# RMSNorm with SiLU on one core: all block transfers through one queue, in turns of loads and stores

## The chip, the core and the metric

The kernel runs on one core of a Trainium2 chip. The core has engines that run side by side, each with its own list of instructions: VectorE (DVE in the profile), ScalarE (ACT), TensorE (PE), GpSimd (POOL) and SyncE (SP), which here only issues transfers. Data lies in HBM and is worked on in SBUF, an on-chip memory of 128 partitions; 16 DMA engines carry it between the two. A transfer is issued by an instruction on an engine's list (here SyncE's or ScalarE's), goes into that engine's DMA queue, and is then carried out while the engine goes on. An instruction that must wait for a semaphore holds up all that stands behind it on its engine.

The metric is device time in microseconds (us). A profiled execution shows every instruction and every DMA packet.

## The reference

```python
batch, seq_len, hidden = 8, 1024, 2048        # x: float32
rms = np.sqrt(np.mean(x ** 2, axis=-1, keepdims=True) + eps)
out = gamma * x / rms
return (out * (1 / (1 + np.exp(-out)))).astype(np.float32)
```

That is 8192 rows of 2048 numbers. Each row is divided by its root mean square, multiplied by gamma, and put through SiLU. 64 MiB are read and 64 MiB written.

## The kernel before

The rows are cut into 16 blocks of 512 rows (`nblk`). A block is one SBUF tile of 128 partitions with four rows each (`J = 4`): 32 KB a partition, 4 MiB in all. Partition p of block b holds four neighbouring rows, so that a block is one contiguous piece of HBM. The pool has six such tiles (`BUFS = 6`); a block is loaded into one, worked on in place, and stored from it, and the block six later takes it over when the store has landed.

The steps of a block b, with the lines of the profile:

- `load(b)`, line 54: a transfer issued by ScalarE.
- `squares_scalar(b)`, line 65, and `squares_vector(b)`, line 73: the sums of squares of its four rows, some on ScalarE (Square with a running sum), the others on VectorE (a multiply with a sum, called reduce below). `share(b)` says how many ScalarE takes: two, or one for the even blocks from 4 to 12.
- `root(b)`, line 82: Sqrt on ScalarE over the four sums. Before it ScalarE loads the table with Sqrt, unless it has it already; Square needs no other table than the one that is there.
- `invert(b)`, line 87: the reciprocal, on VectorE.
- `multiply(b)`, line 92: four instructions on VectorE, x times the row's reciprocal times gamma.
- `silu(b)`, line 98: its table, then two instructions on ScalarE, two rows each; then `store(b)`, line 102: a transfer issued by SyncE.

So loads pass through ScalarE's DMA queue (q10 in the profile) and stores through SyncE's (q1). The order on each engine is the order of the text, since the schedule is written by hand (`manual_schedule`).

The start: load 0, gamma's row (8 KB, line 110, by SyncE), load 1; TensorE spreads gamma over the partitions by a multiplication with ones (line 113), VectorE copies it to SBUF (line 115), and a small copy on ScalarE (line 116) waits for that. Behind it on ScalarE come loads 2 to 5.

The main loop, for b from 0 to 14, has three forms. In the first three turns: multiply(b), the squares of block b+1 on ScalarE, silu(b) and its store, the squares of b+1 on VectorE, root(b+1), invert(b+1). From turn 3 to 13: squares and root of b+1 first, then multiply(b), silu(b) and the store, invert(b+1). Here a load, `[b + 3]`, is issued on ScalarE after the first Square of block b+1, for blocks 6 to 15; it waits until the store of the block six before has landed. Turn 14 has the first form again. The last block's rows are multiplied by gamma alone (line 155) and the reciprocal is applied as the scale of four Silu instructions (line 157), each ready for one row; then its store.

Of the kernel before, what the change touches and what calls it, by code (L numbers as in the profile page):

```python
# [1 line left out]

# [4 lines left out]

ACT = mybir.ActivationFunctionType
ALU = mybir.AluOpType


@with_exitstack
def kernel(
    ctx: ExitStack,
    tc: tile.TileContext,
    x: bass.AP,
    gamma: bass.AP,
    eps: bass.AP,
    out: bass.AP,
):  # L20

    nc = tc.nc
    P = nc.NUM_PARTITIONS
    f32 = mybir.dt.float32
    x2 = x.flatten_outer_dims()
    o2 = out.flatten_outer_dims()  # L30
    n, d = x2.shape
    J = 4
    BUFS = 6
    nblk = n // (P * J)
    xb = x2.rearrange("(b p j) d -> b p (j d)", p=P, j=J)
    ob = o2.rearrange("(b p j) d -> b p (j d)", p=P, j=J)

    singles = ctx.enter_context(tc.tile_pool(name="singles", bufs=1))
    pool = ctx.enter_context(tc.tile_pool(name="pool", bufs=BUFS))
    small = ctx.enter_context(tc.tile_pool(name="small", bufs=2))  # L40
    psum = ctx.enter_context(tc.tile_pool(name="psum", bufs=1, space=bass.MemoryType.PSUM))

    Q = 4
    w = d // Q
    g = singles.tile([P, d], f32)
    eps_t = singles.tile([P, 1], f32)
    ones = singles.tile([P, P], f32)
    junk_a = psum.tile([P, d], f32, name="junk_a")
    junk_v = psum.tile([P, d], f32, name="junk_v")
    blocks, sss, rmss, rstds = {}, {}, {}, {}  # L50

    def load(b):
        xt = pool.tile([P, J * d], f32, name="xt")
        nc.scalar.dma_start(out=xt, in_=xb[b])  # L54
        blocks[b] = xt

    def row(b, j):
        return blocks[b][:, j * d:(j + 1) * d]

    def squares_scalar(b, loads=()):  # L60


        sss[b] = small.tile([P, J], f32, name="ss")
        for j in range(share(b)):
            nc.scalar.activation(out=junk_a, in_=row(b, j), func=ACT.Square,  # L65
                                 accum_out=sss[b][:, j:j + 1])
            if j == 0:
                for s in loads:
                    load(s)

    def squares_vector(b):
        for j in range(share(b), J):
            nc.vector.tensor_tensor_reduce(  # L73
                out=junk_v, in0=row(b, j), in1=row(b, j), scale=1.0, scalar=0.0,
                op0=ALU.mult, op1=ALU.add, accum_out=sss[b][:, j:j + 1])

    def share(b):
        return 1 if 4 <= b <= 12 and b % 2 == 0 else 2

    def root(b):  # L80
        rms = small.tile([P, J], f32, name="rms")
        nc.scalar.activation(out=rms, in_=sss.pop(b), func=ACT.Sqrt, scale=1.0 / d, bias=eps_t)  # L82
        rmss[b] = rms

    def invert(b):
        rstd = small.tile([P, J], f32, name="rstd")
        nc.vector.reciprocal(out=rstd, in_=rmss.pop(b))  # L87
        rstds[b] = rstd

    def multiply(b):  # L90
        for j in range(J):
            nc.vector.scalar_tensor_tensor(out=row(b, j), in0=row(b, j), scalar=rstds[b][:, j:j + 1],  # L92
                                           in1=g, op0=ALU.mult, op1=ALU.mult)

    def silu(b):
        for h in range(0, J, 2):
            cols = slice(h * d, (h + 2) * d)
            nc.scalar.activation(out=blocks[b][:, cols], in_=blocks[b][:, cols], func=ACT.Silu)  # L98
        store(b)

    def store(b):
        nc.sync.dma_start(out=ob[b], in_=blocks[b])

    with tc.manual_schedule():

        load(0)
        nc.vector.memset(ones, 1.0)  # L107
        nc.vector.memset(eps_t, float(eps))
        nc.scalar.activation(out=junk_a[:, 0:1], in_=ones[:, 0:1], func=ACT.Square)  # L109
        nc.sync.dma_start(out=g[0:1, :], in_=bass.AP(tensor=gamma.tensor, offset=gamma.offset, ap=[[d, 1], [1, d]]))  # L110
        for c in range(Q):
            cols = slice(c * w, (c + 1) * w)
            nc.tensor.matmul(junk_v[:, cols], ones[0:1, :], g[0:1, cols], start=True, stop=True)  # L113
        load(1)
        nc.vector.tensor_copy(out=g, in_=junk_v)  # L115
        nc.scalar.copy(out=junk_a[:, 0:1], in_=junk_v[:, d - 1:d])  # L116
        for b in range(2, BUFS):
            load(b)

        last = nblk - 1
        SOON = 3
        squares_scalar(0)
        squares_vector(0)
        root(0)
        invert(0)
        for b in range(last):
            loads = [b + 3] if BUFS <= b + 3 < nblk else []
            if b < SOON:  # L130
                multiply(b)
                squares_scalar(b + 1, loads)
                silu(b)
                squares_vector(b + 1)
                root(b + 1)
            elif b < last - 1:
                squares_scalar(b + 1, loads)
                squares_vector(b + 1)
                root(b + 1)
                multiply(b)  # L140
                silu(b)
            else:
                multiply(b)
                squares_scalar(b + 1)
                silu(b)
                squares_vector(b + 1)
                root(b + 1)
            if b + 1 < last:
                invert(b + 1)


        for j in range(J):
            if j == J // 2:
                invert(last)
            nc.vector.tensor_mul(out=row(last, j), in0=row(last, j), in1=g)  # L155
        for j in range(J):
            nc.scalar.activation(out=row(last, j), in_=row(last, j), func=ACT.Silu,  # L157
                                 scale=rstds[last][:, j:j + 1])
        store(last)


# [1 line left out]
_INS = ['x', 'gamma', 'eps']  # L163
_OUTS = [((8, 1024, 2048), 'float32')]

_NUMBERS = {'eps': 9.999999747378752e-06}


# [26 lines left out]
```

## Time and profile before

| | us |
|---|---|
| three runs: lowest, median, highest | 316.79, 317.0, 317.33 |
| profiled execution, first to last instruction (span) | 315.1 |
| median of the runs less that span | 1.9 |
| VectorE busy | 235.3 (75%) |
| ScalarE busy | 213.9 (68%) |
| PE busy | 7.2 (2%) |
| moved by DMA | 134.24 MB, 426 GB/s over the span |
| a load from issue to landing, median | 38.7 |
| a store from issue to landing, median | 29.0 |

The profile's page gives, for each engine, its busy time, and for 40 equal slices of the span the busy tenths of each engine, the busy share of the 16 DMA engines, and the rate of the packets that start in the slice. Its chain is the work that ended last, followed back from the end: at each step to what released it. Groups of instructions are shown with line, engine, operation, output<-inputs, shapes and count, then busy time, mean ns of one, the idle time of the engine just before them and what ended it. Windows give busy times and the DMA rate of chosen stretches, in us from the span's start; packets are counted in the window in which they start.

### The profile page before, as it was taken

What the parts mean: (1) busy time and instruction counts of PE and PEld (TensorE: products, weight loads), DVE (VectorE), ACT (ScalarE), POOL (GpSimd) and SP (SyncE); (2) the same over time, 40 slices, a digit from 0 to 9 for tenths busy, and PEclk for the clock granted to TensorE, in tenths of its full rate; (3) what the DMA queues carried; (4) which work ended last, traced back from release to release, by engine and by line L of the source; (5) the groups of instructions that cost most, each with busy time, mean ns of one, the idle gap of its engine ahead of it and who ended that gap; (6) DMA issues with size and microseconds to landing.
All of it is one profiled execution on the core that took longest, in us unless ns stands there. A gap on an engine that the chain in (4) does not pass through costs nothing.

```text
span 315.1 us, 439 instructions
## 1 busy us (share of the span) xinstructions
PE 7.2 (2%) x8; PEld 2.5 (1%) x8; DVE 235.3 (75%) x157; ACT 213.9 (68%) x137; POOL 0.2 (0%) x4
## 2 busy tenths in 40 slices
PE   6200000000000000000000000000000000000000
PEld 2000000000000000000000000000000000000000
DVE  0679697979895695957969489593995939999600
ACT  1269998972799258682687827877278768779910
POOL 0000000000000000000000000000000000000000
DMA  8999999999999999999999999999999999999997
GB/s 334 412 453 416 383 458 408 462 403 462 403 459 408 454 412 458 408 462 403 462 403 462 408 458 408 458 408 458 416 449 416 449 416 449 428 437 428 437 428 308
DMA packets 4613, 134.24 MB, mean 426 GB/s; under 512 B 514, under 2 KB 514, under 8 KB 514
## 3 DMA queue, kind: packets, MB, share of 16 engines
q10 hardware_dynamic: 2304, 67.11, 49.8%
q1 hardware_dynamic: 2306, 67.12, 49.3%
q14 instruction: 3, 0.02, 0.0%
HBM read 67.12 MB, written 67.11 MB: 426 GB/s over the span
## 4 chain that ended last, share of the span: by engine, by line
DMA 68%; DVE 14%; ACT 11%; issue 1%; ACTq 1%; DVEq 0%
DMA xt<-in_x_dram 68%; DVE xt L92 9%; DVE junk_v L73 5%; ACT xt L98 4%; ACT junk_a L65 3%; ACT xt L157 2%; ACT L82 1%; ACTq L190 1%; ACT L157 0%; ACT L98 0%; ACT rms L82 0%; DVE ss L73 0%; ACTq L54 0%; DVE rstd L87 0%; ACT L109 0%
## 5 line engine op out<-in xcount | busy, mean ns | idle before, releaser
L92 DVE SCALAR_TENSOR_TENSOR xt<-xt,rstd,g 128x2048 f32<-128x2048 f32 x60 | 137.0, 2346 | 0.1
L98 ACT ACTIVATE xt<-xt 128x4096 f32<-128x4096 f32 x30 | 108.3, 3615 | 27.4 <-DVE xt L92 27.4
L73 DVE CUSTOM_DVE_ANT_0 junk_v<-xt 128x2048 f32<-128x2048 f32 x37 | 85.1, 2299 | 42.9 <-DMA xt<-in_x_dram 42.2
L65 ACT ACTIVATE junk_a<-xt 128x2048 f32<-128x2048 f32 x27 | 50.7, 1876 | 16.1 <-DMA xt<-in_x_dram 14.0
L82 ACT ACT_TABLE_LOAD x15 | 19.2, 1283 | 26.6 <-DVE ss L73 26.5
L98 ACT ACT_TABLE_LOAD x14 | 18.0, 1283 | 0.2
L115 DVE COPY g<-junk_v 128x2048 f32<-128x2048 f32 x1 | 2.3, 2292 | 9.0 <-PE junk_v L113 9.0
L87 DVE RECIPROCAL rstd<-rms 128x4 f32<-128x4 f32 x16 | 2.7, 172 | 8.4 <-ACT rms L82 8.4
L155 DVE TENSOR_TENSOR xt<-xt,g 128x2048 f32<-128x2048 f32 x4 | 8.9, 2277 | 0.0
L82 ACT ACTIVATE rms<-ss,eps_t 128x4 f32<-128x4 f32 x16 | 4.8, 297 | 5.7 <-DVE ss L73 5.5
L157 ACT ACTIVATE xt<-xt,rstd 128x2048 f32<-128x2048 f32 x4 | 7.7, 1991 | 0.0
L113 PE MATMUL junk_v<-g,ones 1*128 1x512 f32 x8 | 7.2, 1072 | 2.8 <-DMA g<-in_gamma_dram 2.8
L116 ACT COPY junk_a<-junk_v 128x1 f32<-128x1 f32 x1 | 0.1, 144 | 9.8 <-DVE g L115 9.8
L73 DVE DVE_READ_ACCUMULATOR2_ANT ss<- 128x1 f32 x37 | 5.2, 141 | 0.0
L65 ACT ACTIVATION_READ_ACCUMULATOR junk_a<-xt 128x1 f32 x27 | 5.0, 186 | 0.0
L113 PEld LDWEIGHTS junk_v<-g,ones 1*128 1x128 f32 x8 | 2.5, 325 | 5.9 <-issue 5.9
L109 ACT ACT_TABLE_LOAD x1 | 1.3, 1283 | 1.1 <-PEq L176 1.1
L157 ACT ACT_TABLE_LOAD x1 | 1.3, 1283 | 0.0
L107 DVE MEMSET ones<- 128x128 f32 x1 | 0.2, 165 | 0.8 <-PEq L176 0.8
L109 ACT ACTIVATE junk_a<-ones 128x1 f32<-128x1 f32 x1 | 0.2, 174 | 0.0
L176 POOL MEMSET const-bfloat16-1.0<- 128x1 bf16 x1 | 0.1, 103 | 0.0
L176 POOL MEMSET const-uint8-127<- 128x1 uint8 x1 | 0.1, 102 | 0.0
(3 smaller groups left out, 0.3 us busy)
## 6 DMA issues: line engine op xcount, KB each, us to landing
xt<-in_x_dram ACTq DMA_DIRECT2D x16, 4096.0 KB, 38.7
out_dram<-xt SPq DMA_DIRECT2D x16, 4096.0 KB, 29.0
g<-in_gamma_dram SPq DMA_DIRECT2D x1, 8.0 KB
```

What stands on the lines that cost most here:

```text
L65: nc.scalar.activation(out=junk_a, in_=row(b, j), func=ACT.Square, accum_out=sss[b][:, j:j + 1])
L73: nc.vector.tensor_tensor_reduce(out=junk_v, in0=row(b, j), in1=row(b, j), scale=1.0, scalar=0.0, op0=ALU.mult, op1=ALU.add, accum_out=sss ...
L82: nc.scalar.activation(out=rms, in_=sss.pop(b), func=ACT.Sqrt, scale=1.0 / d, bias=eps_t)
L87: nc.vector.reciprocal(out=rstd, in_=rmss.pop(b))
L92: nc.vector.scalar_tensor_tensor(out=row(b, j), in0=row(b, j), scalar=rstds[b][:, j:j + 1], in1=g, op0=ALU.mult, op1=ALU.mult)
L98: nc.scalar.activation(out=blocks[b][:, cols], in_=blocks[b][:, cols], func=ACT.Silu)
L109: nc.scalar.activation(out=junk_a[:, 0:1], in_=ones[:, 0:1], func=ACT.Square)
L113: nc.tensor.matmul(junk_v[:, cols], ones[0:1, :], g[0:1, cols], start=True, stop=True)
L115: nc.vector.tensor_copy(out=g, in_=junk_v)
L155: nc.vector.tensor_mul(out=row(last, j), in0=row(last, j), in1=g)
L157: nc.scalar.activation(out=row(last, j), in_=row(last, j), func=ACT.Silu, scale=rstds[last][:, j:j + 1])
L190: with _tile.TileContext(nc) as tc:
```

## The change

All 32 block transfers are issued by SyncE, in an order written out in `QUEUE`: loads 0 to 5, stores 0 to 4, loads 6 to 10, stores 5 to 9, loads 11 to 15, stores 10 to 15. `transfers(done)`, called after the Silu of each block, issues the next entries of that list as far as they are loads or stores of blocks that are done in the text; each still waits on its semaphores, a store for its Silu, a load for the landing of the store that had its slot. Gamma's row is issued by ScalarE instead of SyncE. The small copy on ScalarE is gone.

The six tiles become six slots of one tile, `ring`. Blocks are paired: partition p holds eight neighbouring rows of a pair, four in the even block and four in the odd one (`view`), so that the rows of one block's neighbouring partitions stand 64 KB apart in HBM instead of 32 KB; each partition's piece is 32 KB as before.

The compute order goes by groups of blocks (0 to 5, 6 to 10, 11 to 15). The first block of a group has no look-ahead but the squares of the next on ScalarE and VectorE around its Silu; within the group the squares of block b+1 stand before the multiply of b; but the group's last block is worked on after the Silu of the one before it, except block 15. ScalarE and VectorE take two rows of squares each in every block. The small buffers for sums and roots are three instead of two.

```diff
+QUEUE = [
+    ('L', 0), ('L', 1), ('L', 2), ('L', 3), ('L', 4), ('L', 5),
+    ('S', 0), ('S', 1), ('S', 2), ('S', 3), ('S', 4),
+    ('L', 6), ('L', 7), ('L', 8), ('L', 9), ('L', 10),
+    ('S', 5), ('S', 6), ('S', 7), ('S', 8), ('S', 9),
+    ('L', 11), ('L', 12), ('L', 13), ('L', 14), ('L', 15),
+    ('S', 10), ('S', 11), ('S', 12), ('S', 13), ('S', 14), ('S', 15),
+]
+
+GROUPS = [range(0, 6), range(6, 11), range(11, 16)]
...
-    pool = ctx.enter_context(tc.tile_pool(name="pool", bufs=BUFS))
-    small = ctx.enter_context(tc.tile_pool(name="small", bufs=2))
+    small = ctx.enter_context(tc.tile_pool(name="small", bufs=3))
...
+    ring = singles.tile([P, SLOTS * J * d], f32, name="xt")
...
-    def load(b):
-        xt = pool.tile([P, J * d], f32, name="xt")
-        nc.scalar.dma_start(out=xt, in_=xb[b])
-        blocks[b] = xt
+    def rows(b, j, k):
+        at = (b % SLOTS) * J + j
+        return ring[:, at * d:(at + k) * d]
...
+    def view(t, blocks):
+
+        q = blocks[0] // 2
+        both = t[q * 2 * P * J:(q + 1) * 2 * P * J, :].rearrange("(p j) d -> p (j d)", p=P, j=2 * J)
+        at = blocks[0] % 2 * J
+        return both[:, at * d:(at + len(blocks) * J) * d]
+
+    todo = list(QUEUE)
+
+    def transfer():
+        kind, *blocks = todo.pop(0)
+        sb = rows(blocks[0], 0, len(blocks) * J)
+        if kind == "L":
+            nc.sync.dma_start(out=sb, in_=view(x2, blocks))
+        else:
+            nc.sync.dma_start(out=view(o2, blocks), in_=sb)
+
+    def transfers(done):
+
+        while todo and (todo[0][0] == "L" or todo[0][-1] <= done):
+            transfer()
...
-    def share(b):
-        return 1 if 4 <= b <= 12 and b % 2 == 0 else 2
+    def squares(b):
+        squares_scalar(b)
+        squares_vector(b)
+        root(b)
...
-        store(b)
-
-    def store(b):
-        nc.sync.dma_start(out=ob[b], in_=blocks[b])
+        transfers(b)
...
-        load(0)
+        transfer()
...
+        nc.scalar.dma_start(out=g[0:1, :], in_=bass.AP(tensor=gamma.tensor, offset=gamma.offset, ap=[[d, 1], [1, d]]))
...
-        nc.sync.dma_start(out=g[0:1, :], in_=bass.AP(tensor=gamma.tensor, offset=gamma.offset, ap=[[d, 1], [1, d]]))
...
-        load(1)
+        transfer()
         nc.vector.tensor_copy(out=g, in_=junk_v)
-        nc.scalar.copy(out=junk_a[:, 0:1], in_=junk_v[:, d - 1:d])
-        for b in range(2, BUFS):
-            load(b)
...
+        transfers(-1)
+
+        for group in GROUPS:
+            first, end = group[0], group[-1]
+            squares(first)
+            invert(first)
+            multiply(first)
+            squares_scalar(first + 1)
+            silu(first)
+            squares_vector(first + 1)
+            root(first + 1)
+            for b in group[1:-1]:
+                if b + 1 < end or end == last:
+                    squares(b + 1)
+                invert(b)
                 multiply(b)
                 silu(b)
...
+            if end < last:
+                squares(end)
+                invert(end)
+                multiply(end)
+                silu(end)
...
-        store(last)
+        transfers(last)
```

## The prediction

> **What bounds the kernel now.** I read the page's slices and queues first, then the chain that ended last, then the rate of the transfers stretch by stretch, and last the engines. The page:
>
> ```profile
> DMA  8999999999999999999999999999999999999997
> ...
> DMA packets 4613, 134.24 MB, mean 426 GB/s; under 512 B 514, under 2 KB 514, under 8 KB 514
> ...
> q10 hardware_dynamic: 2304, 67.11, 49.8%
> q1 hardware_dynamic: 2306, 67.12, 49.3%
> ...
> DMA 68%; DVE 14%; ACT 11%; issue 1%; ACTq 1%; DVEq 0%
> ...
> L92 DVE SCALAR_TENSOR_TENSOR xt<-xt,rstd,g 128x2048 f32<-128x2048 f32 x60 | 137.0, 2346 | 0.1
> L98 ACT ACTIVATE xt<-xt 128x4096 f32<-128x4096 f32 x30 | 108.3, 3615 | 27.4 <-DVE xt L92 27.4
> L73 DVE CUSTOM_DVE_ANT_0 junk_v<-xt 128x2048 f32<-128x2048 f32 x37 | 85.1, 2299 | 42.9 <-DMA xt<-in_x_dram 42.2
> L65 ACT ACTIVATE junk_a<-xt 128x2048 f32<-128x2048 f32 x27 | 50.7, 1876 | 16.1 <-DMA xt<-in_x_dram 14.0
> ```
>
> The 16 DMA engines are at 9 in every slice but the first and last; the two queues' packets take 49.8 + 49.3 = 99.1% of their span. The chain is 68% a load being waited for, and VectorE and ScalarE stand 42.2 and 14.0 us for loads. So the transfers are the bound: 16 blocks in, 16 out, 4 MiB each. The windows tell what rate they get (time, busy time of PE, PEld, DVE, ACT, POOL, clock, DMA share, GB/s):
>
> ```profile
> 4.50:34.90 30.40, 5.44 (x7) 1.66 (x5) 20.95 (x14) 17.89 (x14) 0.00 (x0) 1.00 1.00 431
> 34.90:40.75 5.85, 0.00 (x0) 0.00 (x0) 3.92 (x3) 5.77 (x8) 0.00 (x0) 1.00 0.98 358
> 40.75:279.20 238.45, 0.00 (x0) 0.00 (x0) 192.98 (x129) 167.21 (x102) 0.00 (x0) 1.00 1.00 433
> ...
> 279.20:312.00 32.80, 0.00 (x0) 0.00 (x0) 17.26 (x11) 21.56 (x13) 0.00 (x0) 1.00 1.01 435
> ```
>
> The first stretch is loads alone (the first store is issued at 35.18 in the timeline), the third is both directions at once from two queues, the last is stores alone (the last load is through at 279.2 in the chain). The three rates are the same: packets are counted where they start, and one round of 16 packets of 32 KB is 0.52 MB, 1.2 us of a stretch. Direction and number of queues do not change the rate. The one hole is the second stretch, in which the store queue starts beside the running load queue:
>
> ```profile
> DMA packets 64, 2.10 MB, mean 358 GB/s; under 512 B 0, under 2 KB 0, under 8 KB 0
> ```
>
> 2.10 MB at 433 GB/s would be 4.84 us; it took 5.85. 1.0 us is lost there, once. All the rest at 433 GB/s is 134.24 MB, 309.9 us. SyncE's wait for the last store ends at about 314.1 (the issue, the last of line 102, starts at 300.9 and is over by 301.2; the wait behind it is 12.9). 314.1 - 309.9 = 4.2 us is thus all that stands above the rate: the 1.0, some 2.5 at the start (first issue at 0.73, next to nothing moved before 1.7, and 374 GB/s from 1.7 to 4.5), and the rest the last landing.
>
> **The change, part by part**, against the profiled execution (span 315.1). The runs' median, 317.0, is 1.9 above that span; I keep the 1.9.
>
> *Bytes and packets.* 16 loads and 16 stores of 4 MiB in 32 KB pieces stay: 309.9 us at the measured rate. With one direction at a time the rows above give 431 and 435 against 433 mixed: no gain, no loss. Cost 0; the error of these windows is about one round of packets in 30 us, and the long one pins the mixed rate, so I allow 0.3% (1 us) either way for it.
>
> *The start.* Load 0 is now SyncE's first instruction; SyncE issued gamma at 0.73, the same time as ScalarE its load. Gamma goes to ScalarE's queue, ahead of its table load. 0. Loads 2 to 5 were issued at 12.38, behind ScalarE's copy; now they follow at once (six issues of about 0.4 to 0.5 us). They wait in the queue behind loads 0 and 1 either way, so nothing lands earlier. ScalarE loses the copy (0.14), the waits behind it, and its four issues (1.81): its first Square starts at about 13.0 instead of 14.29, off the path.
>
> *Does the one queue ever run dry?* SyncE issues in order, so a store that waits for its Silu holds up every later transfer. Working it out from rows: two reduces 2 x 2.4, reciprocal 0.2, four multiplies 4 x 2.35 make VectorE 14.4 a block; two Squares 4.0, two table loads 2.6, Sqrt 0.3, two Silus 7.2 make ScalarE 14.1. Load 0 lands at 0.73 + 12.2 = 12.9, and as before store 0 is ready at 35.2 (block 0 and 1 keep their order). VectorE, whose multiply of block 0 ends near 29, then does two pairs of reduces and the multiply of block 1 (end 47.9), and goes on at 14.4: stores are ready 3.7 after each multiply, at 51.6, 65.8, 80.0, and store 4 at 89.4 (block 5's reduces come after it).
> The queue: the chain has load 1 through at 22.66; with 9.69 us a block (4.194 MB at 433 GB/s) load 5 is through at 61.4, and stores 0 to 4 end at 71.1, 80.8, 90.5, 100.2, 109.9. Each must be issued about 1 us before its turn: store 3 is ready at 80.0 for 90.5, store 4 at 89.4 for 100.2. The least lead is some 10 us.
> Loads 6 to 10 wait in SyncE for their slot's store to land (71.1 to 109.9) and for store 4's issue; load 6 is queued at 90 for 109.9, load 10 at 111 for 148.6. They end at 119.6 to 158.3. Store 5 (ready at 108) is queued at 111. Block 6 landed, the same pattern as from 12.9 to 35.2 gives store 6 at 141.9, then 158.3, 172.5, and store 9 at 181.9 for its turn at 197.1. Loads 11 to 15 end at 216.4 to 255.2, stores 11 to 14 are ready at 238.7, 255.1, 269.3, 283.5 for 264.9, 274.6, 284.3, 294.0. Block 15: from 279.8 four gamma multiplies of 2.28 and four Silus of 1.99 behind them end at 292.6, for 303.7. So every wait on compute lies under a transfer of another block: 0. What covers it is the 10 us of lead; each us of lateness beyond that would be a us at the end. The look-ahead, the dropped uneven share of squares and the extra small buffers (3 for 2) act only within it.
> The last store ends at 255.2 + 6 x 9.69 = 313.3, against 314.1 now.
>
> *The hole at 34.9.* It is where the second queue starts. Now only one queue carries blocks, and its stores are queued 25 us before their turn. Bounds: it goes (-1.0), or it belongs to the first store, whichever queue, and comes again at 61 (0). I take -1.0: what is slow in that stretch is not the stores but two rounds of loads ahead of them (from 36 to 39.5 the windows have 32 packets start, all of the load queue, with 94.3% of the engines' time: 1.65 us each), and a queue's start costs something at 1.7 to 4.5 too (2.8 us x (1 - 374/433) = 0.4).
>
> *Five turns of direction* (61, 110, 158, 207, 255). No row shows a load behind a store in one queue. Lower end 0: from 40.75 to 279.2 the engines serve both queues, half and half, at the single-direction rate. Upper end: each turn costs what the hole did, 5 x 1.0 = 5.0; the 0.4 of the first start lies between, 2.0 for five. I take 0, the long row being nearest.
>
> *Addresses.* A block's partition rows are now 64 KB apart in HBM instead of 32 KB, two blocks interleaved; each piece stays 32 KB. No row has that spacing. Ends: 0, since no row shows the HBM side setting the rate; or the slowest rate of any row, 358 GB/s, throughout: 375 - 310 = +65. I take 0, by the kinship with the 32 KB pieces of all rows.
> The Trainium skill speaks against this part: "DMA: Bandwidth & Descriptors", section "Latency and other measured facts", has copies whose rows in HBM lie a large power of two apart run slower, 207 GB/s a direction at 512 KiB against 214 at full rate. By that 3% the sum would be some 10 us more, about 326; its smallest spacing is eight times the one here, and no row of this profile tests it.
>
> **Sum:** 315.1 - 1.0 + 0 + 0 = 314.1 span, 316.0 with the 1.9 around it.
>
> **The rivals.**
> A (0.45), the forecast: the hole goes, turns are free: 316.0, own range 315.6 to 316.6.
> B (0.23), the hole stays, as it belongs to the first store: 317.0. For it: it happens just when stores begin. Against: it stretches loads.
> C (0.15), on the slower side: each turn of direction in one queue empties the engines for p. The end is 316.0 + 5p; it is slower by 0.2% from p = 0.33. At 0.4 it is 318.0, at 1.0 it is 321.0. For it: the hole is the only place where a direction begins. Against: 238 us of both directions at 433.
> D (0.08), the 64 KB spacing costs rate: each 1% is 3.1 us; 319 to 326.
> E (0.05), a store comes later than its turn, because compute loses its 10 us of lead: for 2 to 4 us in one turn, 318 to 320. Against: VectorE and ScalarE now stand 42.2 and 14.0 us for loads.
> F (0.04), one direction at a time is faster than mixed: 0.5% of 309.9 is 1.5 us: 314.5. Against: 431 and 435.
>
> **How the numbers follow.** About 0.2% (0.6 us) can be told from no change. Faster: most of A (0.38) and F, 0.42. Same: the rest of A and most of B, 0.28. Slower: C, D, E and a little of B, 0.30. The range from 315.6 to 319.8 holds A, B, most of C and E and the low part of D, some 0.85; F, the far half of C and most of D lie outside.
>
> **What the profile would show.** Right: one queue with nearly all bytes, the other only gamma; 433 GB/s in each turn and no dip at 61, 110, 158, 207, 255; stores issued near 35, 52, 66, 80, 89, and the last near 293; engines' waits for loads large, with no effect. Wrong: dips at the turns (C), one near 61 only (B), a rate below 430 inside a turn (D), or a store issued after the transfer before it has ended (E).

## The result, and the profile after

The changed kernel takes 317.44 us (median of 16 runs, 317.2 to 318.13) against 317.0 before (16 runs, 316.79 to 317.33); the ratio is 1.0018, with a 95% interval of 1.0011 to 1.0024. It is slower, by 0.4 us, where 1.0 us less was forecast. The profiled execution has a span of 316.3, and it is the slowest of the 16 (318.13); the median run's span is 315.7, so 0.6 us of what its trace shows more than before is its own.

The page of the changed kernel (slices, queues, chain, groups):

```profile
DMA  8999999999999999999999999999999999999996
...
DMA packets 4612, 134.24 MB, mean 424 GB/s; under 512 B 513, under 2 KB 513, under 8 KB 513
...
q1 hardware_dynamic: 4608, 134.22, 98.9%
...
q10 hardware_dynamic: 2, 0.01, 0.0%
...
DVE 58%; DMA 25%; ACT 6%; issue 1%; DVEq 1%; ACTq 1%; SPq 0%
...
L96 DVE CUSTOM_DVE_ANT_0 junk_v<-xt 128x2048 f32<-128x2048 f32 x32 | 73.5, 2298 | 40.3 <-DMA xt<-in_x_dram 39.6
L91 ACT ACTIVATE junk_a<-xt 128x2048 f32<-128x2048 f32 x32 | 60.0, 1876 | 52.1 <-DMA xt<-in_x_dram 51.6
```

The bytes are in one queue now, and the DMA engines are as full as before. The chain names VectorE with 58%, but that is the way it is followed: a store in the queue was released by its Silu long before its turn, and the chain goes back from there. VectorE and ScalarE still stand idle 39.6 and 51.6 us for loads. The bound is the same, so the places to look are those where the engines moved less than their 433 GB/s. The windows of the changed kernel (columns as in the prediction, the last is GB/s):

```profile
4.50:58.10 53.60, 5.51 (x7) 1.66 (x5) 45.46 (x31) 39.24 (x31) 0.00 (x0) 1.00 1.00 430
58.10:61.70 3.60, 0.00 (x0) 0.00 (x0) 3.60 (x3) 3.60 (x2) 0.00 (x0) 1.00 1.00 291
61.70:154.00 92.30, 0.00 (x0) 0.00 (x0) 67.44 (x45) 66.33 (x43) 0.00 (x0) 1.00 1.01 435
154.00:162.00 8.00, 0.00 (x0) 0.00 (x0) 7.93 (x7) 7.06 (x5) 0.00 (x0) 1.00 0.98 422
162.00:250.00 88.00, 0.00 (x0) 0.00 (x0) 60.65 (x39) 59.40 (x40) 0.00 (x0) 1.00 1.01 435
250.00:258.00 8.00, 0.00 (x0) 0.00 (x0) 7.93 (x8) 7.09 (x4) 0.00 (x0) 1.00 0.95 406
258.00:312.00 54.00, 0.00 (x0) 0.00 (x0) 31.12 (x18) 33.68 (x22) 0.00 (x0) 1.00 1.01 435
...
135.00:185.00 50.00, 0.00 (x0) 0.00 (x0) 48.17 (x32) 46.31 (x27) 0.00 (x0) 1.00 1.00 431
230.00:280.00 50.00, 0.00 (x0) 0.00 (x0) 49.72 (x33) 48.17 (x32) 0.00 (x0) 1.00 1.01 433
```

Loads alone, stores and loads across a turn, stores alone: full rate in all the long windows. The two short ones at 422 and 406 GB/s lie round the second and the third turn from loads to stores; windows of 50 us there, 135 to 185 and 230 to 280, have 431 and 433, so on the mean over the engines a turn loses 0.2 us there at most, and the rest of what the short ones miss is where they are cut. The exception is the stretch from 58.1 to 61.7. There 32 pieces (a piece is a packet of 32 KB), 1.05 MB, start in 3.60 us; at 433 GB/s they would need 2.42. The hole did not go: it moved from 35 to the first turn, and is 1.2 us instead of 1.0. The stores were not late. From 35 on they were issued as the prediction has them, the fourth and fifth with 10 us in hand (the timeline, SyncE; start, length):

```profile
35.03 0.35 SPq L81 DMA_DIRECT2D out_dram<-xt  x1
51.09 0.34 SPq L81 DMA_DIRECT2D out_dram<-xt  x1
65.06 0.33 SPq L81 DMA_DIRECT2D out_dram<-xt  x1
79.03 0.33 SPq L81 DMA_DIRECT2D out_dram<-xt  x1
88.08 0.33 SPq L81 DMA_DIRECT2D out_dram<-xt  x1
```

The end differs too. These are the packets that start after 312.8, in the kernel before and then in the changed one (the 16 small ones, called notes below, hold 4 bytes each; each of the 32 block transfers ends with 16 of them, which fits one for each DMA engine that is done with its share):

```profile
DMA packets 16, 0.00 MB, mean 0 GB/s; under 512 B 16, under 2 KB 16, under 8 KB 16
```

```profile
DMA packets 22, 0.20 MB, mean 47 GB/s; under 512 B 16, under 2 KB 16, under 8 KB 16
```

Before, all pieces are under way by then. In this execution of the changed kernel six more start, the last one some 0.9 us after the other five: one of the 16 engines is a piece behind. So there are two things to find out: what the hole is, and whether turns cost anything.

### The profile page after: what moved, and what is told of

The parts are those of the page before. It is cut to its first block, busy times and chain, and to the rows that moved or that the text cites. A ratio compares the mean times of both kernels' runs of the same rounds, so it can differ in the third digit from the quotient of the medians.

```text
span 316.3 us, 423 instructions
## 1 busy us (share of the span) xinstructions
PE 7.2 (2%) x8; PEld 2.5 (1%) x8; DVE 224.3 (71%) x147; ACT 217.9 (69%) x142; POOL 0.2 (0%) x4
## 4 chain that ended last, share of the span: by engine, by line
DVE 58%; DMA 25%; ACT 6%; issue 1%; DVEq 1%; ACTq 1%; SPq 0%
DVE xt L117 37%; DMA xt<-in_x_dram 25%; DVE junk_v L96 19%; ACT xt L122 2%; ACT xt L165 2%; DVE xt L163 1%; ACT L107 1%; DVEq L198 1%; DVE ss L96 1%; ACTq L198 1%; DVE rstd L112 0%; ACT rms L107 0%; SPq L81 0%; ACTq L107 0%; DVEq L96 0%
## 5 line engine op out<-in xcount | busy, mean ns | idle before, releaser
L96 DVE CUSTOM_DVE_ANT_0 junk_v<-xt 128x2048 f32<-128x2048 f32 x32 | 73.5, 2298 | 40.3 <-DMA xt<-in_x_dram 39.6
L91 ACT ACTIVATE junk_a<-xt 128x2048 f32<-128x2048 f32 x32 | 60.0, 1876 | 52.1 <-DMA xt<-in_x_dram 51.6
L112 DVE RECIPROCAL rstd<-rms 128x4 f32<-128x4 f32 x16 | 2.8, 174 | 14.2 <-ACT rms L107 14.2
L91 ACT ACTIVATION_READ_ACCUMULATOR junk_a<-xt 128x1 f32 x32 | 6.0, 186 | 0.0
L96 DVE DVE_READ_ACCUMULATOR2_ANT ss<- 128x1 f32 x32 | 4.5, 140 | 0.0
```

What stands on the lines that cost most here:

```text
L96: nc.vector.tensor_tensor_reduce(out=junk_v, in0=row(b, j), in1=row(b, j), scale=1.0, scalar=0.0, op0=ALU.mult, op1=ALU.add, accum_out=sss ...
```

## What the hole is

Theory W: the first write to the output is slow, whichever queue brings it. Theory T: the first turn from loads to stores in one queue empties the engines. Theory B: it belongs to the first large store, one of 32 KB pieces. And the prediction's own reading, that it is the start of a second queue, is already weak, since the changed kernel has one queue. The first runs put a small store early into the changed kernel, into the output and into another tensor, and into the kernel before.

```diff
 e1: the changed kernel
         nc.vector.memset(eps_t, float(eps))
+        nc.sync.dma_start(out=view(o2, [last])[:, 0:P], in_=ones)
 e2: the same line, into HBM that is not the output
+    scratch = nc.dram_tensor("scratch", (P, P), f32).ap()
...
+        nc.sync.dma_start(out=scratch, in_=ones)
 e5: the same line, into block 0's rows
+        nc.sync.dma_start(out=view(o2, [0])[:, 0:P], in_=ones)
```

> The changed kernel with one more store, 512 B a partition (64 KB) into the last block's rows of the output, issued right behind load 0. The changed kernel lost some 1.2 us around 58, in the last loads before the first store. Theory W (the first write to the output is slow, once, whichever queue brings it): the hole at 58 goes; where the small store comes, in the first 5 us, some 0 to 1 us is lost instead; 316.3 to 317.3. Theory T (the first turn from loads to stores in one queue empties the engines): the hole at 58 stays as it is, 317.4 to 317.7. Theory B (the hole belongs to the first large store of 32 KB pieces): the hole at 58 stays too.

> The changed kernel with one more store of 64 KB, at the same place as in the run before, but into a scratch tensor in HBM that is not the output. If the hole at 58 belongs to the first write by any queue to HBM or to the first read of SBUF by a DMA, it goes as in that run, 316.3 to 317.3. If it belongs to the output tensor's own addresses, it stays, 1.2 us, 317.4 to 317.7. Theories T and B: it stays.

> The changed kernel with the extra store of 64 KB, 512 B a partition, into the rows of block 0 of the output, those that the first large store writes at 60. The same store into the last block's rows left the hole at 58 to 60 in place (0.9 us). If the hole is the first write to these addresses, it goes: 0.9 us less, 316.6 to 316.9. If it belongs to the first large store, whatever its addresses, it stays: 317.4 to 317.8.

Measured: 317.67, 317.70 and 317.66 (ratios to the kernel before 1.0022, 1.0027 and 1.0026). The hole stays in all three. Windows around it of the first and the third:

```profile
58.20:61.50 3.30, 0.00 (x0) 0.00 (x0) 3.30 (x3) 3.30 (x1) 0.00 (x0) 1.00 1.01 318
```

```profile
58.20:61.50 3.30, 0.00 (x0) 0.00 (x0) 3.30 (x3) 3.30 (x1) 0.00 (x0) 1.00 1.01 318
```

32 pieces in 3.30 us, 0.9 lost; in the second it is 3.40 us, 1.0 lost. Theory W falls: a first write, to the output or elsewhere, does not take the hole along when its pieces are 512 B. (The third run wrote only the first 512 B of each 32 KB piece of block 0; that the other addresses don't matter either follows from the next two.) The small store is also a turn from loads to stores in the queue, the first one, and the hole did not come at it. Then one full block, and one round of 32 KB pieces, one for each engine, were stored early, one execution each:

```diff
 e6: the changed kernel, behind the second load
         transfer()
+        nc.sync.dma_start(out=view(o2, [last]), in_=rows(0, 0, J))
 f4: the same line with 16 partitions
+        nc.sync.dma_start(out=view(o2, [last])[0:16, :], in_=rows(0, 0, J)[0:16, :])
```

> The changed kernel with a store of 4 MiB more, of the raw block 0 out of its slot into the last block's rows of the output, issued when load 0 has landed, so that it runs behind load 1, from about 22 to 32. The last block's own store overwrites it at the end. It costs 9.7 us of transfer: 326.5 to 328. If the hole belongs to the first large store, whichever it is, about 1 us is lost just before 22 and nothing when store 0's turn comes near 70. If it belongs to block 0's addresses, or to a first turn after six loads in a row, the hole is near 70, and none near 22.

> The changed kernel with one store more behind load 1: the raw rows of block 0 from 16 partitions only, 32 KB each, one piece for each DMA engine (0.5 MB, 1.2 us of transfer), into the last block's rows of the output, overwritten at the end. A full block stored at this place took the hole of 1.2 us with it and left 0.2 at store 0. If a single round of 32 KB pieces suffices, about 1 us is lost near 22 beside the 1.2 of transfer, and nothing much near 62. If it takes more bytes or more partitions, the hole stays near 60.

Measured 327.42 and 319.52. With one round, the windows around the early store and around store 0:

```profile
15.30:29.80 14.50, 0.00 (x0) 0.00 (x0) 7.25 (x6) 8.53 (x10) 0.00 (x0) 1.00 1.01 400
53.00:67.50 14.50, 0.00 (x0) 0.00 (x0) 14.43 (x10) 14.41 (x10) 0.00 (x0) 1.00 1.01 434
```

14.5 us at 433 GB/s are 6.28 MB; 5.80 were started in the first, which is 1.1 us lost, and 6.29 in the second, nothing lost. So a single round of 32 KB pieces, into the last block's rows, takes the hole with it, and the turn to store 0 has none of it once that is done. By itself this doesn't part theory B from theory T, since the early round is now the queue's first turn to large stores; the kernel before, in which no queue turns between loads and stores of blocks, does that below. The full block had the same: 1.05 MB in the 3.30 us from 20.8, 0.9 lost, and 428 GB/s (0.2 us) in the 15 us around store 0's turn. The time is the sum: one round costs 1.2 us of transfer, and 319.52 is 2.1 above the changed kernel; the remaining 0.9 is not explained by the hole, which was there anyway. It fits a late engine: the notes of the last store are 2.3 us apart in this trace, against 1.0 to 1.6 in three traces of the changed kernel.

Has the kernel before the same hole for the same reason? Three edits of it, the first two with one execution each:

```diff
 g3: one round of 32 KB pieces out of SBUF, once load 0 has landed
         load(1)
+        nc.sync.dma_start(out=ob[nblk - 1][0:16, :], in_=blocks[0][0:16, :])
 g1: one round from HBM to HBM, behind gamma
+        nc.sync.dma_start(out=ob[nblk - 1][0:16, :], in_=xb[nblk - 1][0:16, :])
 g4: block 0's store in 8 KB pieces
     def store(b):
+        if b == 0:
+            for j in range(J):
+                nc.sync.dma_start(out=ob[b][:, j * d:(j + 1) * d], in_=row(b, j))
+            return
```

> The kernel before, with one round of 32 KB pieces stored from SBUF (the raw rows of block 0 on 16 partitions) by SyncE when load 0 has landed, at about 13. In the one-queue form such a round took the hole with it. If the hole at 36 to 40 of the kernel before is the same thing, it goes from there and 0.9 to 1.2 us are lost between 13 and 18, beside 1.2 us of transfer: 318.0 to 318.5. If the hole of the kernel before is the start of a second queue with many pieces, it stays at 36 to 40.

> The kernel before, with one transfer more on SyncE behind gamma: 16 pieces of 32 KB from the input straight to the output in HBM (the last block's first 16 partitions, overwritten at the end), which reads no SBUF. If what is slow is the first write of 32 KB pieces to HBM, the hole at 36 to 40 (0.9 us) goes, and something is lost in the first 6 us instead, beside 1.2 us of transfer: 317.3 to 318.3. If it is the first read of 32 KB pieces out of SBUF by the DMA engines, the hole stays at 36 to 40, and the whole costs its 1.2 us and more: 318 to 319.

> The kernel before with its first block stored in four transfers of one row each, 8 KB pieces, and all others as they were. If the hole comes with the first 32 KB pieces, it is not at 36 to 40 but near 50, where block 1's store follows, and the time is as before, 316.8 to 317.2. If it comes with the first store of a whole block in whatever pieces, it stays at 36 to 40, same time. If smaller pieces take it away altogether, 316.0 to 316.3.

Measured 319.41, 318.51 and 317.88 (the last with a ratio of 1.0029, 1.0017 to 1.0041). The first one's windows, where the kernel before has its 358 GB/s and where the round was put:

```profile
34.90:40.75 5.85, 0.00 (x0) 0.00 (x0) 3.11 (x6) 5.82 (x5) 0.00 (x0) 1.00 1.01 431
13.10:27.00 13.90, 0.00 (x0) 0.00 (x0) 7.93 (x7) 6.29 (x7) 0.00 (x0) 1.00 1.01 391
```

The hole is gone from 34.9 to 40.75 (431 for 358), though the store queue starts its full blocks there as before; 5.44 MB in 13.9 us are 1.3 us lost at 13 to 27. So it acts as the hole of the changed kernel does, and in this kernel each queue carries blocks one way only: theory T falls. (The time is above its forecast, and 2.5 above the kernel before: 1.2 of transfer, 0.3 by which the hole is larger, and 1.0 that the hole doesn't explain; the last store's notes are 1.6 us apart here, against 0.8.) With the pieces from HBM to HBM the hole stays at its place:

```profile
33.95:41.85 7.90, 0.00 (x0) 0.00 (x0) 4.58 (x5) 7.82 (x7) 0.00 (x0) 1.00 1.00 394
```

3.11 MB in 7.90 us, 0.7 lost, and at most 0.3 from 4.5 to 36.3, where those pieces went (13.63 MB): a first round of large writes to HBM does not take the hole, a first round of large reads out of SBUF does. SyncE's queue had carried a round of 32 KB pieces by 11 in this run, beside the loads, so the start of a second queue with large pieces is not what makes the hole; and the changed kernel has it with one queue. The 8 KB pieces did not do what any of the theories had: 0.5 us is lost from 33 to 47 (5.83 MB), block 0's store drags on (in that window the loads have 162 packets and 4.78 MB, the stores 136 and 1.05 MB), block 1's store of 32 KB pieces passes at full rate (436 GB/s from 69 to 84), and a stretch like the hole comes only after it, ahead of block 2's store:

```profile
84.60:86.90 2.30, 0.00 (x0) 0.00 (x0) 2.27 (x3) 2.30 (x1) 0.00 (x0) 1.00 0.95 256
```

0.59 MB in 2.30 us is 0.9 lost. So this run speaks against the plain form of theory B, that the first 32 KB pieces stored make the hole: they passed without it. What exactly calls for it, size of the pieces, bytes or number of transfers, stays open, and so does the mechanism.

The kernel before with the small early store belongs here as a failure of its own:

```diff
 e4: the kernel before
         nc.vector.memset(eps_t, float(eps))
+        nc.sync.dma_start(out=ob[nblk - 1][:, 0:P], in_=ones)
```

> The kernel before, with one store of 64 KB into the last block's rows of the output issued by SyncE at the start, ahead of gamma. Theory W: the hole at 34.9 to 40.75 (1.0 us by the windows) goes, and what comes in its place at the start is 0 to 1 us: 316.0 to 317.0. A theory that the hole comes when a second queue starts with large packets: it stays, 317.0 to 317.2.

Measured 323.1, ratio 1.0201 (1.0187 to 1.0214). The small store does not take the hole here either (412 GB/s from 44 to 56, 0.6 us lost, where the first large store now begins); the time comes from something else. Gamma's row stands behind the 64 KB in SyncE's queue, and comes so late that TensorE starts on it at 17.01 instead of 2.78; the small copy on ScalarE waits for it, and loads 2 to 5 wait behind that copy. They are issued at 26.61 instead of 12.38, and the DMA engines run dry:

```profile
20.00:24.00 4.00, 4.00 (x5) 1.03 (x4) 0.00 (x0) 0.00 (x0) 0.00 (x0) 1.00 0.34 147
24.00:28.00 4.00, 0.17 (x1) 0.00 (x0) 3.52 (x2) 0.14 (x1) 0.00 (x0) 1.00 0.40 106
28.00:32.00 4.00, 0.00 (x0) 0.00 (x0) 3.49 (x4) 3.37 (x3) 0.00 (x0) 1.00 0.75 319
```

## Where the 0.4 us come from: spacing or turns

```diff
 e3, f1: the changed kernel with contiguous blocks
-        q = blocks[0] // 2
-        both = t[q * 2 * P * J:(q + 1) * 2 * P * J, :].rearrange("(p j) d -> p (j d)", p=P, j=2 * J)
-        at = blocks[0] % 2 * J
-        return both[:, at * d:(at + len(blocks) * J) * d]
+        b = blocks[0]
+        return t[b * P * J:(b + 1) * P * J, :].rearrange("(p j) d -> p (j d)", p=P, j=J)
 e7, f2: the changed kernel, unaltered
 e8: the kernel before with paired blocks
-    xb = x2.rearrange("(b p j) d -> b p (j d)", p=P, j=J)
+    xp = x2.rearrange("(b p j) d -> b p (j d)", p=P, j=2 * J)
+    xb = [xp[b // 2][:, b % 2 * J * d:(b % 2 + 1) * J * d] for b in range(nblk)]
... and ob likewise
```

> The changed kernel with each block contiguous in HBM again (rows of neighbouring partitions 32 KB apart, not 64 KB); all else as changed. If the spacing has a part in the 0.3 us by which the hole is larger than before (1.2 against 0.9), and in the 0.1 us lost near 254, the hole shrinks to 0.9 and the time to 317.0 to 317.1. If it has none (the size comes from the queue or the turn), 317.4 as changed. If the spacing costs rate throughout, which the trace of the changed kernel denies, more than 0.5 us is gained.

> The changed kernel once more, unaltered, on the same chip as the next one and with the kernel before, to have the size of the difference and of the hole a second time: 317.2 to 317.6, ratio 1.001 to 1.0025, a hole of 0.9 to 1.2 us near 58.

> The kernel before with the blocks paired in HBM as in the change (rows of neighbouring partitions 64 KB apart), and nothing else: two queues as before. If the spacing is what makes the changed kernel slower by 0.3 to 0.4 us (the contiguous form of the changed kernel took 317.11 against its 317.44), this is slower by as much: 317.2 to 317.4. If the one queue in turns is what does it, 316.9 to 317.1.

> The changed kernel with contiguous blocks a second time, now on the same chip as the changed kernel itself (next run). If the spacing has its 0.3 us in the one-queue form (317.11 on one chip against 317.44 and 317.63 on others), this is 0.3 to 0.5 us below the next run; if the difference was one between chips, they agree within 0.15 us.

> The changed kernel, unaltered, beside the contiguous form: 317.3 to 317.7 by what it did twice.

| run | us | kernel before, same chip | ratio, 95% interval |
|---|---|---|---|
| e3 contiguous | 317.11 | 316.94 | 1.0014 (1.0003 to 1.0024) |
| e7 changed | 317.63 | 316.89 | 1.0022 (1.0013 to 1.0030) |
| e8 before, paired | 317.03 | 316.89 | 1.0005 (0.9996 to 1.0013) |
| f1 contiguous | 317.30 | 316.91 | 1.0014 (1.0005 to 1.0022) |
| f2 changed | 317.38 | 316.91 | 1.0015 (1.0006 to 1.0024) |

The first contiguous run looked like a gain of 0.3 us; beside the changed kernel on one chip the two agree within 0.08. In two queues the spacing makes no difference that can be told (e8). So the form with one queue is slower, 0.14 to 0.22%, with either spacing. That this is the queue and not the new compute order is argued from the stores' lead; no run changed the compute order alone. The hole may be smaller with contiguous blocks: from 52.3 to 66.9 their two traces have 415 and 408 GB/s, three traces of the changed kernel 400 to 404, which is 0.6 and 0.8 us lost against 1.0 to 1.1; the times don't show it.

Then the number of turns, with one queue and paired blocks as changed:

```diff
 f3: a store and a load in turns (11 turns from loads to stores)
-QUEUE = [
...
-GROUPS = [range(0, 6), range(6, 11), range(11, 16)]
+QUEUE = [('L', 0), ('L', 1), ('L', 2), ('L', 3), ('L', 4), ('L', 5), ('S', 0)]
+for n in range(6, 16):
+    QUEUE += [('S', n - 5), ('L', n)]
+QUEUE += [('S', 11), ('S', 12), ('S', 13), ('S', 14), ('S', 15)]
+GROUPS = [range(0, 16)]
 g2: two stores and two loads in turns (6), all else as in f3
...
+for n in range(6, 16, 2):
+    QUEUE += [('S', n - 5), ('S', n - 4), ('L', n), ('L', n + 1)]
...
```

> The changed kernel with the same one queue and paired blocks, but after six loads and a store the order is a store and a load in turns (10 loads, each behind a store), so that there are 11 turns from loads to stores instead of 3; the groups of the compute order become one group of 16. The trace of the changed kernel shows 1.2 us lost at its first such turn, 0 at the second and 0.1 at the third. If a turn costs nothing by itself and only the first large store does, 317.2 to 317.8. If a later turn costs 0.1 to 0.2 us on the mean or holds up single engines, eight more cost 0.8 to 1.6 us or more: 318.2 to 319.5.

> As the alternating order in the run before, but two stores and two loads in turns, which makes 6 turns from loads to stores; the changed kernel has 3 and takes 317.4, one by one has 11 and took 320.9. If each such turn costs the end 0.44 us (3.5 us over 8 turns), 318.7, between 318.2 and 319.2. If the loss of the alternating order came from something else, as the landing of a store that a load waits for with only one transfer queued behind it, two by two has it less or not at all: 317.3 to 317.8.

Measured 320.91 (ratio 1.0128, 1.0112 to 1.0143) and 319.31 (1.0076, 1.0060 to 1.0093). With 3, 6 and 11 turns the time is 317.4, 319.3 and 320.9: every turn more costs, 0.6 us each up to 6 and 0.3 each from there, 0.44 on the mean. The forecast for 6, 318.2 to 319.2, was just missed on the far side. The queue does not run dry for it. Of the alternating order, a window over all its turns, and the packets after 312.8; then these packets of two by two:

```profile
61.70:312.00 250.30, 0.00 (x0) 0.00 (x0) 174.77 (x113) 179.54 (x113) 0.00 (x0) 1.00 1.00 432
```

```profile
DMA packets 29, 0.43 MB, mean 69 GB/s; under 512 B 16, under 2 KB 16, under 8 KB 16
```

```profile
DMA packets 21, 0.16 MB, mean 26 GB/s; under 512 B 16, under 2 KB 16, under 8 KB 16
```

Against the 435 GB/s that the changed kernel has behind its hole, 432 over 250 us is 1.7 us at most on the mean over the engines; the median time is 3.5 us longer, more than either theory had (this traced execution is the fastest of the four, 320.06). The second line has the rest: 13 pieces start after 312.8 (0.43 MB), where the kernel before has none, spread over some 3 us. Two by two has 21 packets and 0.16 MB there, five pieces. The notes of the last store, in us from the span's start, say the same more plainly:

| trace | turns from loads to stores | first note | last note | span |
|---|---|---|---|---|
| before | none, two queues | 313.1 | 314.0 | 315.1 |
| f2 changed | 3 | 313.3 | 314.5 | 315.7 |
| g2 two by two | 6 | 313.3 | 316.3 | 317.5 |
| f3 one by one | 11 | 313.3 | 317.1 | 318.3 |

The first engine is done at the same time within 0.2 us in all four; the last one is not, and the span ends 1.2 us behind it in each. So single engines fall behind, and the last one sets the end.

The notes of the blocks in between show where. In the two by two trace the first and the last note of a transfer are apart by 1.4 us for loads 7 and 8, 2.0 for loads 9 and 10, 2.7 for loads 11 and 12, and 3.0 from load 13 on; for the two stores between such loads they are as far apart as for the load before them. So where the distance grows, it grows from the first to the second load of a pair, in the load that stands just ahead of stores, and never at a turn from stores to loads. One by one has 1.0 for load 6 and 3.7 for load 15, and there too each step comes with a load and none with a store behind it. In four of five traces with three turns (changed or contiguous) the distance grows by 0.2 to 0.9 at load 15, ahead of the third turn, and in the fifth by 0.1; at load 10, ahead of the second, by 0.1 at most. It is the turn from loads to stores that leaves engines behind, then, by an amount that differs from turn to turn; why is not shown.

## Why the prediction was wrong

**The rate: right.** It took 433 GB/s whatever the direction; loads alone have 430, stores 435. Rival F, one direction at a time as faster, is out.

**The queue never dry: right.** Stores ready at 35.2, 51.6, 65.8, 80.0, 89.4 by the sum were issued at 35.03, 51.09, 65.06, 79.03, 88.08, the last at 292.55 for 292.6. (The sum goes on in steps of 14.2, though the rows that it names add up to 14.4; measured are 13.97.) The 10 us of lead were there, and rival E did not come.

**The hole at 34.9: this step failed.** The prediction said "It is where the second queue starts" and took -1.0, with 0 as the other end. The runs put rival B in its place, as far as the place goes: the hole of 1.0 to 1.2 us came ahead of the first store, in one queue as in two, and one early round of 32 KB pieces stored out of SBUF takes it away in both (f4, g3), while such a round from HBM to HBM in the second queue does not (g1). What in the first stores makes it stays open (g4). The clue that misled was that the slow pieces before were loads and not the store's own. Of the 1.4 us between 316.0 and 317.44 this is 1.0, and up to 0.2 more, since the hole of the changed kernel has 0.9 to 1.2 us in its traces.

**Five turns: mis-sized.** Taken as 0, between 0 and 1.0 each. The long mixed row was the wrong kin: there both queues run side by side and the last store's notes are 0.8 us apart, while in one queue a turn from loads to stores costs 0.44 us at the end by the orders with more of them. The two turns from loads to stores behind the first would have 0.9 by that; the changed kernel shows 0.2 to 0.7, which is what its three comparisons have above the kernel before (0.44, 0.74 and 0.47) with or without 0.2 for the larger hole. So rival C has its mechanism half right: single engines and not all of them, at the turns from loads to stores and not at those back, and a smaller size in this order.

**Addresses: right**, 0. The rule weighed there, from the Trainium skill's "DMA: Bandwidth & Descriptors", section "Latency and other measured facts", on large power-of-two spacings in HBM, names none below 512 KiB. No effect is seen at 64 KB: paired against contiguous is 1.0005 (0.9996 to 1.0013) in two queues, and 317.38 against 317.30 in one.

**The chances:** of the 0.42 on faster, 0.38 rested on the hole alone, a stretch of 5.85 us with no second instance in the trace. One event that is seen once doesn't bear that.

No form tried beats the kernel before.

## What to carry to other kernels

Where transfers are the bound and full, look for what is left in windows of a few rounds of packets, and ask of a hole what else begins there before giving it to the nearest cause: here two things began at once. Rows of two queues that run side by side are no price for turns within one queue. When the end is set by 16 engines, a mean rate doesn't show a late one; the packets that start in the last few microseconds do, and so does the distance between the first and the last note of each transfer.

## What the hardware showed that was not expected

About 0.6 to 1.3 us are lost once in a run, around the first round of 32 KB pieces that DMA reads out of SBUF (in one form, whose first store had 8 KB pieces, only ahead of its third, after one of 32 KB pieces had passed without it); 512 B pieces don't take it along, nor do 32 KB pieces from HBM to HBM (0.7 us still lost at the old place).

Turns from loads to stores in one queue leave single DMA engines behind: 3.5 us at the end for 8 turns more, at 432 GB/s on the mean. With the same blocks in two queues the last store's notes are 0.8 us apart (1.3 in the paired form), against 3.7. The Trainium skill's "DMA: Bandwidth & Descriptors", section "Issuing engines are not separate DMA queues", says that transfers from several engines interleave on the same 16 DMA engines and that issuing from several saves only issue time. The rate agrees (433 GB/s either way). That nothing but issue time is saved does not: two queues were 0.14 to 0.22% faster than one in turns, and 1.3% faster than one that alternates.

A transfer of 128 small pieces ahead of gamma in its queue, beside a queue of large loads, held up loads 2 to 5 from 12.38 to 26.61 and cost 6.2 us.
